# Moving the stores of one helper from SP's transfer queue to ScalarE's and GpSimd's

## The chip, the cores and the metric

The kernel runs on one core of a Trainium2 chip. A core has five engines that run their own instruction streams: TensorE (PE in the profile, with its weight loads as PEld), VectorE (DVE), ScalarE (ACT), GpSimd (POOL) and SyncE (SP). SP does no arithmetic here; it issues transfers between HBM and the on-chip buffers. ScalarE and GpSimd can issue transfers too, between their own instructions. The transfers of every issuer are carried out by the core's 16 DMA engines.

The metric is the device time of one execution in microseconds (us). Before the change three runs took 2751.06, 2753.01 and 2756.75 us; the median is 2753.01.

## The reference, cut to what matters

One layer of a hybrid encoder with 2048 tokens and a width of 1024, all in float32:

```python
xn = rms_norm(x, mix_norm_g)
proj = xn @ w_in
aq, ak, av, mq, mk, mv, mo, ipre, fpre, ga, gm = jnp.split(proj, points, axis=-1)
att = chunk_band_attention(aq, ak, av, rel_bias)          # 8 heads of 64, own chunk and 8 before it
hm = mlstm_chunkwise(silu(conv(mq)), silu(conv(mk)), mv, ipre + b_igate, fpre + b_fgate)
mlstm_out = sigmoid(mo) * rms_norm(hm, mh_norm_g)          # 4 heads of 128
y = sigmoid(ga) * (att @ w_att_proj) + sigmoid(gm) * (mlstm_out @ w_mlstm_proj)
x = x + y @ w_out
hn = rms_norm(x, ffn_norm_g)
x = x + jnp.square(jax.nn.relu(hn @ w_up)) @ w_down
return rms_norm(x, final_norm_g)
```

The large matrix products (`w_in`, `w_out`, `w_up`, `w_down`) make up most of the work.

## The kernel before

**Tiling.** The tokens stand in four blocks of 512. A tile is 128 partitions by 512 float32 values, 256 KB. For the precision of float32 every operand of a product is split into a rounded high part and a rest, and each 128 x 128 x 512 step is three matmuls (high x high, high x rest, rest x high). The large products are also built from seven smaller ones instead of eight (a Strassen-like scheme): sums and differences of operand quarters are formed, stored in HBM where they are needed again, and loaded part by part.

**What goes through HBM.** On-chip memory is small for this, so nearly every intermediate is stored and loaded again: the attention's v (`vspill`), q and k (`qfar`, `kfar`), the recurrence's inputs (`mfar`, `mvfar`), the gates (`gate`), partial sums of the input projection (`park`), the mixers' outputs (`mix`), the gated sum y (`yp`), the residual stream (`x`), the sums of operand quarters of the feed-forward's inner activations (`u`), of weights (`wsum`) and of the input (`xu`), and small rows (`mrow`, `gatepart`, `relrow`, `mid`).

**The planner.** The program is not written in the order in which it runs. Every piece of work is a Python generator that yields the engine it wants, the time it expects to take and, for transfers, a time until the data have landed: `yield "sp", 800, 2000` means 800 ns of SP's clock and landing 2000 ns later. The class `Flow` keeps a clock for each engine, picks the piece that can start earliest (then by priority), moves the engine's clock on and lets the generator write its instructions. That fixes the order in each engine's instruction stream; on the chip each stream then runs strictly in order, with semaphores for the true dependencies. So a price in a `yield` changes no instruction by itself, but it changes where that instruction and all later ones stand. `Flow.now` is a pair, the present time of the running piece and the engine on which that time came about. After a `yield "dve", ...` its second part is `"dve"`; a piece that is started by another takes over its pair; a piece that waits for an event takes the later of its own pair and the event's.

**Buffers.** The pools are small: 16 `ctx` tiles and 6 `tmp` tiles of 512 columns, 4 `wraw` tiles for raw weights, 3 `wsp` tiles for split weights, 28 `r` tiles for split operands, 8 banks of matmul results. A tile that is being stored is given back in the plan when the store has landed, and on the chip its next writer waits for that.

**The lines around the change.** `store` (L2041) is the helper for most stores. Its callers: `sum_w` (`wsum`, quarter sums of weights, after VectorE's L438), `park_u2` and `park_v` (`park`, after VectorE), `merge` (`yp`, with the queue given as `"sp!"`, which is SP at the highest priority), `evac_v` and `after_vm` (`vspill`, after VectorE's rest part; `mvfar` after an addition on VectorE), `evac_mv` (`mvfar` of blocks 0 and 1, after ScalarE), `parts` (`qfar` and `kfar`: the high part, written by ScalarE, and the rest, written by VectorE, both stored after the latter), `after_in` (`gate` and the output gate in `mfar`, after a tanh on ScalarE), `conv_far` (`mfar`, after VectorE), `take_x1` (`xu`), `after_up` through `keep` and `sums` (`u`: parts 0 and 1 are sent when ScalarE has squared them, parts 2 to 6 after VectorE's L1855 to L1864), `x2_tile` (`x`, after VectorE's L2004), `norm_mid` (`mid`), `final_keep` (`fin`), `gates_rest` (`mrow`), `gates_kept` (`gatepart`) and `table` (`relrow`).

Stores that do not use the helper: `keep` inside `quad_w` (L515, sums of weights), `keep_mix` (L1298), and the outputs (L2316 on ScalarE's queue, L2319 and L2374 on SP's).

Loads that stand in SP's queue among the stores: weights (L447, L456, L465), the parts of `u`, `xu` and `mix` (`take_u1`, L2103, split by ScalarE's L1109 and VectorE's L1114), quarters for weight sums (L433), parked sums (L769, then added by VectorE's L780), and the operands of attention and recurrence. Weights are split by ScalarE's L501 and VectorE's L503. GpSimd's own work is small: powers of small tiles (L1033, L1055, L1637, L2291, L2391), a select (L1549) and memsets (L1157, L1544).

Of the kernel before, what the change touches and what calls it, by code (L numbers as in the profile page):

```python
# [101 lines left out]
class Flow:  # L102
# [10 lines left out]
               act=dict(pe=220.0, act=130.0, dve=130.0, pool=180.0),  # L113
               dve=dict(pe=220.0, act=130.0, dve=130.0, pool=155.0), pool=dict(pe=290.0, act=130.0, dve=60.0),
               sp=dict())
# [132 lines left out]
class Layer:  # L248
# [1790 lines left out]
        fl.put(self.ctx, x)  # L2039

    def store(self, dst, src, ev, pool=None, item=None, queue="sp"):  # L2041
        yield queue, 800, 2000
        self.nc.sync.dma_start(dst, src)
        self.fl.set(ev)
        if pool is not None:
            self.fl.put(pool, item)
# [517 lines left out]
```

## Time and profile before

| | |
|---|---|
| median of three runs | 2753.01 us |
| the profiled execution | 2753.07 us |
| its span in the trace | 2751.3 us |
| HBM traffic | 458.79 MB read, 212.21 MB written |
| mean DMA rate | 245 GB/s |
| stores and loads issued on SP's queue | nearly all: 670.08 of 673.57 MB |
| ScalarE's queue | 1.06 MB |

The page gives the busy share of each engine over the whole span, and later the chain of work that ended last. Matmuls are pipelined: one 128 x 512 matmul is listed with 390 ns, but in an undisturbed stretch the next one starts about 227 ns later, so the mean time of one is not the pace. In a row of the timeline the columns are start, duration, engine, line, operation, output and inputs, and the count; "SPq" or "ACTq" is an issue of a transfer by that engine's instruction stream, which lasts until the transfer has been handed on, not until it has landed.

### The profile page before, as it was taken

What the parts mean: (1) busy time and instruction counts of PE and PEld (TensorE: products, weight loads), DVE (VectorE), ACT (ScalarE), POOL (GpSimd) and SP (SyncE); (2) the same over time, 40 slices, a digit from 0 to 9 for tenths busy, and PEclk for the clock granted to TensorE, in tenths of its full rate; (3) what the DMA queues carried; (4) which work ended last, traced back from release to release, by engine and by line L of the source; (5) the groups of instructions that cost most, each with busy time, mean ns of one, the idle gap of its engine ahead of it and who ended that gap; (6) DMA issues with size and microseconds to landing.
All of it is one profiled execution on the core that took longest, in us unless ns stands there. A gap on an engine that the chain in (4) does not pass through costs nothing.

```text
span 2751.3 us, 38074 instructions
## 1 busy us (share of the span) xinstructions
PE 2724.6 (99%) x12832; PEld 2261.5 (82%) x12832; DVE 2086.0 (76%) x3689; ACT 1526.4 (55%) x2640; POOL 44.6 (2%) x79
## 2 busy tenths in 40 slices
PE   9999999999999999999999999999999999999998
PEld 8878888788888887888888888888888888888887
DVE  7878776888775778897768889888888665667675
ACT  6545446666652434566556766657345565554443
POOL 0000000000000000000000000000000000000000
PEclk9999999999999999999999999999999999999999
DMA  8877678878877888767668778776864454588863
GB/s 295 284 254 268 234 267 281 260 235 266 255 256 254 299 305 294 244 212 260 246 237 295 254 231 223 239 257 199 294 227 171 151 205 154 180 278 281 283 230 137
DMA packets 331992, 673.57 MB, mean 245 GB/s; under 512 B 36900, under 2 KB 66468, under 8 KB 331796
## 3 DMA queue, kind: packets, MB, share of 16 engines
q1 hardware_dynamic: 331076, 670.08, 72.3%
q8 instruction: 101, 1.65, 0.2%
q10 hardware_dynamic: 720, 1.06, 0.1%
q14 instruction: 95, 0.78, 0.1%
HBM read 458.79 MB, written 212.21 MB: 244 GB/s over the span
## 4 chain that ended last, share of the span: by engine, by line
PE 83%; DVE 7%; DMA 4%; issue 3%; ACT 2%; POOL 0%; SPq 0%; POOLq 0%; DVEq 0%; ACTq 0%
PE bank L631 35%; PE bank L662 9%; PE bank L562 9%; PE bank L564 8%; PE bank L563 8%; PE bank L667 2%; PE bank L1337 2%; PE bank L1262 2%; PE bank L1369 2%; DVE wsp L503 1%; PE bank L856 1%; DVE r L1114 1%; DMA yp<-tmp 1%; DMA r<-u 1%; DVE ctx L1765 1%
## 5 line engine op out<-in xcount | busy, mean ns | idle before, releaser
L631 PE MATMUL bank<-r,wsp 128*128 128x512 f32 x4872 | 1110.9, 390 | 4.2 <-ACT r L1109 1.4
L631 PEld LDWEIGHTS bank<-r,wsp 128*128 128x128 f32 x4872 | 912.5, 188 | 198.2 <-ACT r L1109 2.1
L501 ACT CAST wsp<-wraw 128x1024 fp32r<-128x1024 f32 x439 | 461.3, 1051 | 492.1 <-PE bank L631 183.3
L503 DVE TENSOR_TENSOR wsp<-wraw,wsp 128x1024 fp32r<-128x1024 f32 x439 | 537.0, 1223 | 247.0 <-ACT wsp L501 236.7
L562 PE MATMUL bank<-r,wsp 128*128 128x512 f32 x1088 | 429.9, 396 | 0.3 <-DVE scs L1343 0.3
L564 PE MATMUL bank<-r,wsp 128*128 128x512 f32 x1088 | 425.3, 391 | 0.0
L563 PE MATMUL bank<-r,wsp 128*128 128x512 f32 x1088 | 425.2, 391 | 0.0
L662 PE MATMUL bank<-r,wsp 128*128 128x512 f32 x1512 | 370.8, 394 | 3.1 <-DVE ctx L780 2.5
L662 PEld LDWEIGHTS bank<-r,wsp 128*128 128x128 f32 x1512 | 279.4, 189 | 59.4 <-issue 2.7
L564 PEld LDWEIGHTS bank<-r,wsp 128*128 128x128 f32 x1088 | 204.3, 188 | 43.0
L562 PEld LDWEIGHTS bank<-r,wsp 128*128 128x128 f32 x1088 | 204.5, 188 | 38.4 <-DVE scs L1343 0.7
L563 PEld LDWEIGHTS bank<-r,wsp 128*128 128x128 f32 x1088 | 204.7, 188 | 38.1
L1114 DVE TENSOR_TENSOR r<-r 128x512 fp32r<-128x512 f32 x273 | 181.8, 687 | 56.8 <-ACT r L1109 55.0
L1109 ACT CAST r<-r 128x512 fp32r<-128x512 f32 x273 | 164.7, 621 | 104.4 <-DMA r<-u 77.1
L1798 DVE TENSOR_TENSOR ctx<-bank,ctx 128x512 f32<-128x512 f32 x150 | 103.0, 687 | 64.7 <-PE bank L631 63.6
L520 DVE TENSOR_TENSOR wraw<-wraw,wraw 128x1024 f32<-128x1024 f32 x112 | 136.5, 1220 | 2.2 <-DMA wsum<-wraw 1.0
L1350 ACT ACTIVATE sc<-sc,scs 128x640 f32<-128x640 f32 (+4 forms) x128 | 97.2, 760 | 54.9 <-DVE scs L1343 54.3
L1790 ACT COPY ctx<-bank 128x512 f32<-128x512 f32 x150 | 87.2, 581 | 52.0 <-PE bank L631 50.5
L2119 ACT ACTIVATE ctx<-ctx 128x512 f32<-128x512 f32 x96 | 60.5, 630 | 97.8 <-DVE ctx L1798 97.8
L1374 DVE TENSOR_TENSOR r<-bank,r 128x512 fp32r<-128x512 f32 (+1 forms) x168 | 96.4, 595 | 8.4 <-ACT r L1372 7.5
L1262 PE MATMUL bank<-r,r 128*128 128x512 f32 x336 | 95.7, 367 | 3.5 <-DVE ctx L1674 1.9
L1372 ACT CAST r<-bank 128x512 fp32r<-128x512 f32 (+1 forms) x168 | 80.7, 514 | 27.9 <-PE bank L1369 27.4
(257 smaller groups left out, 3054.1 us busy)
## 6 DMA issues: line engine op xcount, KB each, us to landing
wraw<-in_wf SPq DMA_DIRECT2D x196, 512.0 KB, 4.2
r<-u SPq DMA_DIRECT2D x224, 256.0 KB, 4.4
wraw<-wsum SPq DMA_DIRECT2D x104, 512.0 KB, 4.5
u<-ctx SPq DMA_DIRECT2D x128, 256.0 KB, 2.8
u<-tmp SPq DMA_DIRECT2D x96, 256.0 KB, 2.1
wraw<-in_w SPq DMA_DIRECT2D x47, 512.0 KB, 4.5
ctx<-in_wf SPq DMA_DIRECT2D x88, 256.0 KB, 4.2
wsum<-ctx SPq DMA_DIRECT2D x88, 256.0 KB, 3.1
```

The source lines that it names most:

```text
L501: nc.scalar.copy(w[:, 0], raw)
L503: nc.vector.tensor_sub(w[:, 1], raw, w[:, 0].bitcast(F32))
L520: V.tensor_sub(dst, x, y)
L562: mm(ps, lh, rh, start=first, stop=False)
L563: mm(ps, lh, rl, start=False, stop=False)
L564: mm(ps, ll, rh, start=False, stop=last)
L631: mm(ps, wv[:, x, k, n], a[:, y], start=new and k == 0 and x == y == 0, stop=k == 3 and x == 1, skip_group_check=True)
L662: mm(ps, wv[:, x, k, n], a[:, y], start=start and x == y == 0, stop=stop and x == 1, skip_group_check=True)
L1109: self.nc.scalar.copy(dst[:, 0], src)
L1114: self.nc.vector.tensor_sub(dst[:, 1], src, dst[:, 0].bitcast(F32))
L1262: nc.tensor.matmul(bkv[:, :, c0:c0 + w], st, sl[:, :, o:o + w], start=n == 0, stop=n == total - 1)
L1798: nc.vector.tensor_add(t[:, o:o + 512], ps, t[:, o:o + 512])
```

## The change

`store` looks at the engine on which the running piece's time came about. A store on the default queue whose piece was last on ScalarE (`"act"`) is issued on ScalarE's queue; one whose piece was last on VectorE (`"dve"`) is issued on GpSimd's; any other, and any with another queue given, stays on SP's. The planner's prices change with it: ScalarE gets an empty step with 300 ns of delay, then 60 ns and 2800 ns to landing; GpSimd gets 1000 ns and 2800 ns; SP's were 800 ns and 2000 ns.

```diff
     def store(self, dst, src, ev, pool=None, item=None, queue="sp"):
-        yield queue, 800, 2000
-        self.nc.sync.dma_start(dst, src)
+        if queue == "sp" and self.fl.now[1] == "act":
+            yield "act", 0, 300
+            yield "act", 60, 2800
+            self.nc.scalar.dma_start(dst, src)
+        elif queue == "sp" and self.fl.now[1] == "dve":
+            yield "pool", 1000, 2800
+            self.nc.gpsimd.dma_start(dst, src)
+        else:
+            yield queue, 800, 2000
+            self.nc.sync.dma_start(dst, src)
         self.fl.set(ev)
         if pool is not None:
             self.fl.put(pool, item)
```

## The prediction

> **What bounds the kernel now.** I read the page's busy shares first, then the longest pieces of the chain of waits, then windows of 100 us, and last what TensorE itself waited for.
>
> ```profile
> PE 2724.6 (99%) x12832; PEld 2261.5 (82%) x12832; DVE 2086.0 (76%) x3689; ACT 1526.4 (55%) x2640; POOL 44.6 (2%) x79
> ```
>
> The windows below end at the span, 2751.3 us, so TensorE is idle for 2751.3 - 2724.6 = 26.7 us. A busy share can hide a slow pace, so the second reading is the pace.
>
> ```profile
> 261.53 193.16 PE bank L631 x852
> ```
>
> This piece of the chain of waits is undisturbed: 193.16 / 852 = 0.227 us for a 128x512 product. The windows show whether other stretches keep that pace.
>
> ```profile
> 1000.00:1100.00 100.00, 97.68 (x431) 80.59 (x430) 74.44 (x110) 41.19 (x59) 0.00 (x0) 1.00 0.86 300
> 2300.00:2400.00 100.00, 100.00 (x443) 82.80 (x442) 62.12 (x73) 54.21 (x79) 0.00 (x0) 1.00 0.44 159
> 2700.00:2751.30 51.30, 43.93 (x210) 36.53 (x208) 25.34 (x39) 18.39 (x31) 3.19 (x5) 0.95 0.33 121
> ```
>
> The columns are stretch and length, then busy time (and count) of PE, PEld, DVE, ACT and POOL, then clock, DMA share and GB/s. 443 in 100 us is 0.226 us each; the worst stretch of long products, the first row, has 431, which is 12 x 0.227 = 2.7 us short, at a DMA share of 0.86. The granted clock is 1.00 in both. The last row holds 51.3 - 43.93 = 7.4 us of the idle time; it is the final norm, whose own DMAs do not pass through `store`. The rest is in the list of what TensorE waited for, 21 rows that add to 18.8 us (total us, times, longest):
>
> ```profile
> PE bank L662 <- DVE ctx L780: 2.5, 2, 2.3
> ...
> PE bank L631 <- ACT r L1109: 1.4, 1, 1.4
> ...
> PE bank L1337 <- DVE r L1374: 0.2, 1, 0.2
> ```
>
> So the kernel is bound by TensorE, and 18.8 us (0.7%) is about all that any better feeding could return. What can be lost has no such ceiling.
>
> **What is moved.** One line, 2043, issues every store that passes through `store`, all on SP's queue:
>
> ```profile
> L2043 SPq DMA_DIRECT2D u<-ctx x128: 319/320/792, 1197.8 to 2434.5; - x128
> L2043 SPq DMA_DIRECT2D u<-tmp x96: 319/320/1417, 1224.5 to 2434.1; - x96
> ...
> L2043 SPq DMA_DIRECT2D gate<-ctx x64: 319/320/564, 109.2 to 1098.6; - x64
> L2043 SPq DMA_DIRECT2D mfar<-ctx x48: 319/320/1237, 202.9 to 1110.7; - x48
> ...
> L2043 SPq DMA_DIRECT2D yp<-tmp x32: 319/330/650, 861.0 to 2032.1; - x32
> ...
> L2043 SPq DMA_DIRECT2D mrow<-tmp x4: 270/271/353, 171.4 to 1736.5; - x4
> ...
>   DVE ctx L438: 8.3, 6
> ...
>   DVE wsp L503: 0.2, 1
> ...
> DMA to landing us min/median/max: 2.0/3.0/7.5
> ```
>
> These are the first and the last of 19 rows, which add to 692; four `mid`, one `gatepart` and one `relrow` store make 698. The 32 `yp` stores ask for "sp!" and stay. The planner's last stamp sorts the others. To ScalarE go the gates (64), a third of `mfar` (16, the output gate), `mvfar` of blocks 0 and 1 (8), parts 0 and 1 of the seven of each `u` (2/7 of 224 = 64), `mrow` (4) and `gatepart` (1): 157. To GpSimd go 698 - 32 - 157 = 509, among them the `u` part 6 and the high halves of q and k, whose data ScalarE wrote but whose thread was last on VectorE. Nothing is removed: bytes, transfers and the waits of each store stay.
>
> **SP's queue, which gives up 666 issues.** Each is 0.32 us at the median: 213 us of issuing leave SP, and so do the waits of these stores, which hold back loads written behind them:
>
> ```profile
> SPq L456 <- DVE wsp L503: 229.5, 114, 10.0
> ...
> SPq L2043 <- ACT ctx L2123: 152.7, 80, 9.6
> ```
>
> The first row is SP waiting to load weights until VectorE has let a buffer go: the weights are ahead of their use, so an earlier turn brings nothing there. What the release can return is TensorE's waits for operands whose source is a load: L780 adds a parked tile that is loaded back, L1109 splits a tile that is loaded. They are 2.5 + 1.4 = 3.9 us. Bounds: 0, and 18.8 if all waits vanished. I take -3.9, since the other rows are waits for attention and recurrence work on VectorE and ScalarE that no load starts.
>
> **ScalarE's queue, which gets 157.** The only stores on it in this trace are four of the output:
>
> ```profile
> 2739.49 0.71 ACT L2308 ACTIVATE ctx<-ctx,r_z 128x512 f32<-128x512 f32 x1
> 2739.62 0.35 ACTq L2316 DMA_DIRECT2D out_x<-sc  x1
> 2740.11 0.58 ACT L2298 ACTIVATE tmp<-bank 128x512 f32<-128x512 f32 x1
> ```
>
> The store is issued while the next activation runs, and the one after starts 0.09 us before that ends (2739.49 + 0.71 = 2740.20): no time of ScalarE is lost. The change asks for the same shape: its empty step of 300 ns lets another activation in between. Without that cover ScalarE would wait for its own write and then issue for 0.35 us; behind it stand the casts L501 and L1109, for which L503 and L1114 on VectorE, and then TensorE, wait. Bounds: 0 to 157 x 0.35 = 55 us of an engine that is 55% busy. I take 0; the cover is there in most stages, and 55 us would raise its share only to 57%.
>
> **GpSimd's queue, which gets 509.** No DMA of GpSimd stands in the trace. The nearest row on this engine is a small tensor operation:
>
> ```profile
> L1637 POOL TENSOR_TENSOR hs<-hs,half 128x4 f32<-128x4 f32 x16 | 17.8, 1112 | 231.5 <-DVE hs L1635 194.1 <-DVE scs L1352 37.4
> ```
>
> Bounds for one issue: 0.32 us (SP's) to 1.11 us (a GpSimd instruction). As it is an instruction of that engine I take 1.11, so 0.8 us more per store before its data move; the lower bound is that a store no longer queues behind loads and lands at the 2.0 us minimum, 1.0 us earlier than the median. 509 x 1.11 = 565 us is 21% of the span: GpSimd has room. In its queue the power L1637, the select L1549 and the memsets L1157 and L1544 now stand behind stores that wait for VectorE. One store ahead of each of L1637's 16 operations costs 1.11 us of a recurrence that runs beside TensorE's other products; I count nothing for it (at most 16 x 1.11 = 18 us if no other product were ready).
>
> Which stores are late enough to be seen? The chain of waits passes through five that move, all written last by VectorE:
>
> ```profile
> 77.43 5.87 DMA vspill<-tmp
> ...
> 1006.71 5.22 DMA vspill<-tmp
> ...
> 1075.25 5.25 DMA kfar<-ctx
> ...
> 1143.79 4.60 DMA x<-ctx
> 1149.78 5.75 DMA x<-ctx
> ```
>
> Five at +0.8 us are +4.0 us (bounds -5.0 to +4.0). The chain's `yp` pieces stay on SP. Then there are the buffers: arithmetic engines waited 18 times for a store through `store` to land (the rows from L438's 8.3 us down to L503's 0.2). Each now lands 0.8 us later: 14.4 us more on VectorE and ScalarE, of which I let half, 7.2 us, reach TensorE, because three weight buffers stand between them (bounds 0 and 14.4).
>
> [...]
>
> **The sum.** -3.9 + 0 + 4.0 + 7.2 = +7.3 us. The planner gives every store other prices (60 or 1000 ns on another engine instead of 800 ns on SP), so the written order changes everywhere; that has no row. It can return at most the 18.8 us and may as well double them; I take 0 and widen the range. The profiled execution took 2753.07 us, 1.8 more than its span and equal to the median of 2753.01. Forecast: 2753 + 7 = 2760 us. About 0.2% (5.5 us) is what a measurement of this kernel can tell; the three runs spread by 5.7.
>
> **Rivals.** (1) Faster: the loads were held more than I grant. For it: SP waited 152.7 us at one kind of store alone. Against: TensorE's waits name a load's reader in 3.9 us only. If half of the 18.8 us goes, 9 us: 2744 us. (2) No change: TensorE's lead covers all, gains and delays of a few us cancel: 2753 us. For it: two of the chain's five stores lie in the window that is still 97.68% busy. Against: it is the window with the most idle time of those shown. (3) Much slower: GpSimd's queue in order. A store that waits there for VectorE holds all later ones, and the buffers they free; a store then lands not 0.8 but about 3 us later. The 18 buffer waits and five chain stores make 23 x 3 = 69 us, half of it on TensorE: 35 us, 2788 us. It decides where a wait outlasts the lead of one weight buffer, 24 products x 0.227 = 5.4 us: L438's waits are 8.3 / 6 = 1.4 us now and would be 4.4, two in a row past it. Against it: GpSimd is 2% busy, so its queue is nearly empty. (4) The sorting does not do what it says: if the stamp were "sp" for most stores, nothing would move; but each producer's last step is an arithmetic one, so I give this nothing of its own.
>
> **How the numbers follow.** Forecast 0.42, rival 1 0.22, rival 2 0.16, rival 3 0.20. The forecast's own range is 2753 to 2772 and 0.08 of its chance lies within 0.2%; of rival 1 it is 0.02. So slower is 0.34 + 0.20 = 0.54, same 0.16 + 0.08 + 0.02 = 0.26, faster 0.20. The range reaches from rival 1's centre, less 1 us, to rival 3's, plus 4 us, which leaves about half of each outside: 2743 to 2792.
>
> **What would show it.** Right: 157 issues on ScalarE's queue near 0.35 us with ScalarE's busy time unchanged; 509 on GpSimd's near 1.1 us; these landing about 0.8 us later; TensorE's busy time equal and its idle time at 26.7 + 7 = 34 us, the added waits behind `vspill`, `kfar`, `x` and reused `ctx` and `tmp`. Wrong: TensorE's idle time below 20 us (rival 1); landings 3 us later and VectorE or ScalarE waiting for stores by more than 60 us (rival 3); ScalarE's casts late behind its own stores, which would break the 0 taken there.

## The result and the profile after

| | before | after |
|---|---|---|
| median, us | 2752.66 (4 runs) | 2796.39 (4 runs) |
| lowest to highest, us | 2751.06 to 2756.75 | 2795.35 to 2804.83 |
| span of the profiled execution, us | 2751.3 | 2793.5 |

The kernel became slower by 43.7 us: the ratio is 1.0158, with a 95% interval of 1.0139 to 1.0178. The forecast was 2760 us, and the range ended at 2792.

The busy shares of the page, after:

```profile
PE 2734.8 (98%) x12832; PEld 2266.8 (81%) x12832; DVE 2079.9 (74%) x3684; ACT 1531.1 (55%) x2645; POOL 327.1 (12%) x588
```

TensorE is idle for 2793.5 - 2734.8 = 58.7 us, 32.0 more than before, and busy for 10.2 us more with the same 12832 matmuls. Together these are the 42.2 us of the span. The idle time is in the list of what TensorE waited for (us in total, times, longest), after:

```profile
PE bank L662 <- DVE ctx L780: 13.2, 4, 7.2
PE bank L631 <- DVE ctx L1798: 10.2, 5, 3.7
```

Before, the same two pairs were 2.5 and 1.1 us, so these two rows hold 19.8 of the 32.0 us. L780 and L1798 are VectorE reading results out of the matmul banks, so here TensorE waits for VectorE to empty a bank. The windows of the changed kernel (stretch and length; busy time and count of PE, PEld, DVE, ACT, POOL; clock; DMA share; GB/s) show that VectorE was not busy either:

```profile
200.00:300.00 100.00, 96.29 (x426) 79.49 (x425) 76.12 (x113) 50.06 (x79) 19.82 (x35) 0.98 0.71 247
...
1000.00:1100.00 100.00, 92.82 (x398) 76.29 (x397) 65.93 (x96) 32.90 (x48) 12.44 (x23) 0.95 0.80 277
...
2300.00:2400.00 100.00, 100.00 (x443) 82.81 (x442) 61.76 (x71) 52.75 (x76) 16.22 (x30) 1.00 0.43 153
```

Before, the first of these stretches was full:

```profile
200.00:300.00 100.00, 100.00 (x451) 83.06 (x450) 79.51 (x115) 51.74 (x82) 1.01 (x1) 1.00 0.72 263
```

In the stretch from 1000 to 1100 us 398 matmuls run where 431 ran, and VectorE and ScalarE do less too (65.93 and 32.90 us against 74.44 and 41.19): all three wait. The quiet stretch at 2300 is as before. From 1000 to 1100 us the granted clock is 0.95, against 1.00 before: 9.6 of the 10.2 us of extra busy time are lost pace at such stalls (the last section adds them up).

Who is first in that line of waits? Four views of the changed kernel around its longest stall, TensorE, VectorE, ScalarE and SP in turn (start, duration, what, and in brackets the idle time before it and what ended it):

```profile
1064.10 5.60 PE L662 MATMUL bank<-r,wsp 128*128 128x512 f32 x24
1076.88 15.44 PE L662 MATMUL bank<-r,wsp 128*128 128x512 f32 x55 [7.18 <-DVE ctx L780]
```

```profile
1072.78 0.69 DVE L1116 SCALAR_TENSOR_TENSOR r<-tmp,r 128x512 fp32r<-128x512 f32 x1 [4.52 <-ACT r L1111]
...
1076.06 0.68 DVE L780 TENSOR_TENSOR ctx<-bank,ctx 128x512 f32<-128x512 f32 x1
```

```profile
1064.09 0.63 ACT L1111 ACTIVATE r<-tmp 128x512 fp32r<-128x512 f32 x1 [4.40 <-DMA tmp<-yp]
1066.30 0.63 ACT L1111 ACTIVATE r<-tmp 128x512 fp32r<-128x512 f32 x1 [1.59 <-DMA tmp<-yp]
1072.12 0.63 ACT L1111 ACTIVATE r<-tmp 128x512 fp32r<-128x512 f32 x1 [5.18 <-DMA tmp<-yp]
```

```profile
1056.86 0.32 SPq L2051 DMA_DIRECT2D yp<-tmp  x1
1057.24 7.03 SPq L1715 DMA_DIRECT2D tmp<-yp  x3
1064.37 0.38 SPq L456 DMA_DIRECT2D wraw<-wsum  x1
```

Read from the bottom: SP stores a piece of y and, right behind it, loads y back (three loads that take it 7.03 us, of which 5.7 us are one wait for a stored piece to land); ScalarE waits for these loads, in order, 4.40 + 1.59 + 5.18 us; VectorE's L1116 waits 4.52 us for ScalarE, and the read-out L780 stands behind it; TensorE waits 7.18 us for the bank. Neither GpSimd nor ScalarE's queue is in that chain, and the `yp` stores have not moved. Why, then, did it appear?

### The profile page after: what moved, and what is told of

The parts are those of the page before. It is cut to its first block, busy times and chain, and to the rows that moved or that the text cites. A ratio compares the mean times of both kernels' runs of the same rounds, so it can differ in the third digit from the quotient of the medians.

```text
span 2793.5 us, 38435 instructions
## 1 busy us (share of the span) xinstructions
PE 2734.8 (98%) x12832; PEld 2266.8 (81%) x12832; DVE 2079.9 (74%) x3684; ACT 1531.1 (55%) x2645; POOL 327.1 (12%) x588
## 4 chain that ended last, share of the span: by engine, by line
PE 51%; issue 26%; DVE 9%; DMA 7%; POOL 5%; ACT 2%; SPq 0%; POOLq 0%; ACTq 0%; DVEq 0%
PE bank L631 17%; PE bank L562 6%; PE bank L563 6%; PE bank L564 6%; PE bank L662 5%; DVE wsp L503 2%; PE bank L1262 2%; PE bank L1369 1%; PE bank L1337 1%; DMA r<-u 1%; POOL u L2048 1%; PE bank L856 1%; DVE r L1114 1%; PE bank L667 1%; POOL wsum L2048 1%
## 5 line engine op out<-in xcount | busy, mean ns | idle before, releaser
L631 PE MATMUL bank<-r,wsp 128*128 128x512 f32 x4872 | 1117.2, 390 | 14.8 <-DVE ctx L1798 10.2
L1109 ACT CAST r<-r 128x512 fp32r<-128x512 f32 x273 | 165.3, 621 | 151.6 <-DMA r<-u 128.5
L1798 DVE TENSOR_TENSOR ctx<-bank,ctx 128x512 f32<-128x512 f32 x150 | 102.6, 686 | 61.8 <-PE bank L631 61.0
L1337 PE MATMUL bank<-r,r 128*128 128x256 f32 (+2 forms) x464 | 88.7, 311 | 1.9 <-DMA r<-qfar 1.9
```

What stands on the lines that cost most here:

```text
L631: mm(ps, wv[:, x, k, n], a[:, y], start=new and k == 0 and x == y == 0, stop=k == 3 and x == 1, skip_group_check=True)
L1109: self.nc.scalar.copy(dst[:, 0], src)
L1337: nc.tensor.matmul(bk[:, :c1 - c0], q[:, y, i * P:(i + 1) * P], kf[:, f * P + c0:f * P + c1], start=y == 0, stop=y == 1)
```

## The experiments

Ten kernels were run; each ratio is to the kernel before on the same chip, with a 95% interval.

| run | what leaves SP | order of the instructions | median, us (runs) | ratio |
|---|---|---|---|---|
| e1_act_only | 157 to ScalarE | the build's, new prices | 2765.44 (6) | 1.0034 [1.0022, 1.0047] |
| e2_pool_only | 509 to GpSimd | the build's, new prices | 2795.06 (4) | 1.0136 [1.0115, 1.0156] |
| e3_plan_only | nothing | the build's, new prices | 2778.28 (4) | 1.0078 [1.0061, 1.0094] |
| e4_queues_only | 157 and 509 | the build's, old prices | 2798.71 (4) | 1.0159 [1.0144, 1.0174] |
| e5_pinned_queues | 157 and 509 | held as before, all engines | 2760.76 (10) | 1.0025 [1.0014, 1.0037] |
| e6_pinned_act | all 666 to ScalarE | held as before, all engines | 2775.03 (4) | 1.0072 [1.0051, 1.0093] |
| e7_pinned_pool | 509 to GpSimd | held as before, all engines | 2758.33 (10) | 1.0018 [1.0006, 1.0030] |
| e8_pinned_157 | 157 to ScalarE | held as before, all engines | 2756.95 (11) | 1.0010 [0.9999, 1.0022] |
| e9_pinned_sp | 157 and 509 | held on SP only | 2774.63 (6) | 1.0080 [1.0064, 1.0097] |
| e11_free_sp | 157 and 509 | held on all but SP | 2778.64 (4) | 1.0088 [1.0072, 1.0105] |

The first four tested two theories. P: the planner's new prices (60 or 1000 ns instead of 800 on SP) put the whole program in a worse order. Q: the transfers themselves, issued elsewhere, land later or hold other work.

**e1_act_only: ScalarE's branch alone.** The branch for GpSimd falls to the old one:

```diff
-        elif queue == "sp" and self.fl.now[1] == "dve":
-            yield "pool", 1000, 2800
-            self.nc.gpsimd.dma_start(dst, src)
```

> Only the 157 stores whose piece was last on ScalarE move, with the changed kernel's prices; the 509 others stay on SP. Theory P (the plan: SP's clock no longer carries the stores, so loads and what reads them are written too early): 157 of 666 prices leave SP, so about a quarter of the loss, 2753 + 10 = 2763 us, more where SP was full. Theory Q (the queues: stores land later from GpSimd and share the DMA engines out of turn): GpSimd has nothing, so 2753 us within 5.

Measured: 1.0034, some 9 us.

**e2_pool_only: GpSimd's branch alone.** The same with the other branch left out:

```diff
-        if queue == "sp" and self.fl.now[1] == "act":
-            yield "act", 0, 300
-            yield "act", 60, 2800
-            self.nc.scalar.dma_start(dst, src)
-        elif queue == "sp" and self.fl.now[1] == "dve":
+        if queue == "sp" and self.fl.now[1] == "dve":
```

> Only the 509 stores whose piece was last on VectorE move to GpSimd, with the changed kernel's prices. Theory P: three quarters of the prices leave SP, about 2753 + 33 = 2786 us. Theory Q: GpSimd's stores are the cause, all of it, about 2796 us.

Measured: 1.0136, some 37 us. The 509 stores on GpSimd bring most of the loss; by themselves these two runs do not say how.

**e3_plan_only: the new prices, but SP issues everything.**

```diff
-            self.nc.scalar.dma_start(dst, src)
+            self.nc.sync.dma_start(dst, src)
...
-            self.nc.gpsimd.dma_start(dst, src)
+            self.nc.sync.dma_start(dst, src)
```

> The changed kernel's prices, so the written order of every engine as in the changed kernel, but all stores are issued by SP. Theory P: the order makes the loss: 2790 to 2805 us, and more if SP's real queue is now behind its planned clock. Theory Q: without the other queues the time is as before, 2750 to 2760 us.

Measured: 1.0078, some 21 us, with no transfer moved: another order alone can cost half of the loss. (It is not quite the order of the changed kernel, for a reason that e4 brings out.)

**e4_queues_only: the new queues, but the old prices.**

```diff
+        by = {"act": self.nc.scalar, "dve": self.nc.gpsimd}.get(self.fl.now[1], self.nc.sync)
+        if queue != "sp":
+            by = self.nc.sync
         yield queue, 800, 2000
-        self.nc.sync.dma_start(dst, src)
+        by.dma_start(dst, src)
```

> The prices and so the order of the kernel before (SP's clock, 800 and 2000 ns), but the stores are issued by ScalarE (157) and GpSimd (509). Theory P: 2748 to 2758 us, as before or a little faster because loads no longer stand behind stores. Theory Q: the queues make the loss: 2785 to 2800 us.

Measured: 1.0159, the whole loss without any new price. So P is not needed for a loss of this size, though e3 shows that the new prices by themselves can cost 21 us. Q seemed to stand, until the instruction streams of e4 were laid beside those of before. Although the planner did the same, the streams differ. In the programs that the two kernels build, without the moved stores and the semaphore instructions, 210 of TensorE's 12515 instructions stand in another order, 251 of VectorE's 3694, 161 of ScalarE's 2434 and 239 of the 1598 that SP keeps. The planner does not have the last word, as the description of the kernel before had it: the build places every engine's instructions once more, by its own model of when they are ready, and in the kernel before SP's instructions already stand up to 183 places from where the planner put them. A store that leaves SP changes that model's picture, and with it the order of loads and arithmetic that nobody edited. So two new theories. O: the re-written order costs the time. H: the hardware does (landing times, shared DMA engines, GpSimd's queue in order).

**e5_pinned_queues: the new queues in the old order.** The prices are the old ones; every instruction other than the moved stores is chained to the one that stood ahead of it on its engine before. A list of shifts from the planner's order carries that order:

```diff
+        by = self.fl.now[1] if queue == "sp" else "sp"
         yield queue, 800, 2000
-        self.nc.sync.dma_start(dst, src)
+        self.moving = by in ("act", "dve")
+        {"act": self.nc.scalar, "dve": self.nc.gpsimd}.get(by, self.nc.sync).dma_start(dst, src)
+        self.moving = False
...
+            for e, count in COUNTS.items():
+                got = pinned[e]
+                row = [got[k + shift[at + k]] for k in range(count)]
+                at += count
+                for a, b in zip(row, row[1:]):
+                    tc.add_manual_dep(b, a.name, mybir.DependencyInfo(
+                        mybir.DependencyClass.NoSync, mybir.DependencyReason.DATA), reason="order")
```

> The order of the kernel before is pinned on every engine: all matmuls, all work of VectorE, ScalarE and GpSimd and all loads of SP stand exactly as before; only the 666 stores are issued by ScalarE (157) and GpSimd (509). Theory O (when the stores leave SP, the build writes the loads and their readers in another order, and that order loses): 2748 to 2762 us. Theory H (the transfers themselves: stores of GpSimd land later, and three queues share the DMA engines): 2785 to 2800 us, as the unpinned run with the same prices (2798.7).

Measured: 1.0025, 7 us (4 to 10 by the interval). The same 666 stores from the same two queues, and 37 us of the 44 are gone. The stretches that stalled, in the windows of e5:

```profile
200.00:300.00 100.00, 100.00 (x450) 83.07 (x449) 79.74 (x116) 51.05 (x81) 20.07 (x36) 1.00 0.72 261
...
1000.00:1100.00 100.00, 99.61 (x440) 82.18 (x439) 74.62 (x111) 40.39 (x58) 12.60 (x24) 1.00 0.86 302
```

They are full, with GpSimd issuing as much as in the changed kernel. In the program that e5 builds, every instruction other than the moved stores stands where it stood before. O holds, and H keeps 7 us. Strictly this takes e4 apart, which has the old prices. The changed kernel has the new prices as well; how its own 44 us divide between the order of the prices, the order of the build and the queues was not measured.

**e6_pinned_act and e7_pinned_pool: one queue each, in the old order.** Against e5 only the choice of the queue differs:

```diff
-        {"act": self.nc.scalar, "dve": self.nc.gpsimd}.get(by, self.nc.sync).dma_start(dst, src)
+        (self.nc.scalar if by in ("act", "dve") else self.nc.sync).dma_start(dst, src)
```

```diff
-        {"act": self.nc.scalar, "dve": self.nc.gpsimd}.get(by, self.nc.sync).dma_start(dst, src)
+        (self.nc.gpsimd if by == "dve" else self.nc.sync).dma_start(dst, src)
```

> The same pinned order, but all 666 stores go from ScalarE's queue and none from GpSimd. Theory O: 2748 to 2762 us if ScalarE can carry 666 issues; ScalarE waits for VectorE's results in its own order, so up to 20 us more. Theory H with GpSimd's way of issuing as the cause: near 2753 to 2770 us. Theory H with the second queue as such as the cause: 2785 us or more.

> The same pinned order; the 509 stores go from GpSimd, the 157 of ScalarE stay on SP in their old places. Theory O: 2748 to 2762 us. Theory H: GpSimd's part of the loss, 2780 to 2795 us.

Measured: 1.0072 with all 666 on ScalarE, 1.0018 with 509 on GpSimd. So GpSimd's queue is the cheaper one for these 509 (the other 157 alone cost 0.10% on ScalarE's, in e8). A likely reason, argued and not tested by itself: on ScalarE the casts for the next products stand behind a store that waits for VectorE, on GpSimd little does (in e6 the arithmetic of the two is 1525.0 and 45.6 us).

**e8_pinned_157: only ScalarE's share, in the old order.** The stores that stay on SP are not chained in e7 and e8; 13 of SP's instructions in e7 and 30 in e8 stand elsewhere than before.

```diff
-        {"act": self.nc.scalar, "dve": self.nc.gpsimd}.get(by, self.nc.sync).dma_start(dst, src)
+        (self.nc.scalar if by == "act" else self.nc.sync).dma_start(dst, src)
```

> All five engines keep the order of before; only the 157 stores that ScalarE wrote last leave from ScalarE's queue, the other 509 stay on SP's. Theory O (the re-written order costs about 36 us of the 44, the queues themselves about 7): of the 7 us the 509 on GpSimd alone cost 2758.3 - 2752.6 = 5.8, so these 157 cost 1 to 3 us or nothing: 2752 to 2757 us, no difference that can be told. Rival H (a store issued by ScalarE holds its casts): 157 x 0.33 us is 51 us of ScalarE, half of it seen: 2770 us or more, as the 2775 of all 666 on ScalarE would suggest. A gain of 3 us or more (2750 or less) would say that SP's queue was in the way and the order had hidden it.

Measured: 1.0010 with an interval that takes in 1, against 1.0034 for the same 157 stores in e1, where the order was free and the prices new. No gain came to light: no version here beats the kernel before.

**e9_pinned_sp and e11_free_sp: whose order is it?** In both, the loop of e5 over the engines leaves some out:

```diff
 # e9_pinned_sp
+                if e != "SP":
+                    continue
 # e11_free_sp
+                if e == "SP":
+                    continue
```

> Planner's prices of before, 157 stores on ScalarE's queue and 509 on GpSimd's; SP's remaining transfers are held to the order they had before, the other engines are written as the build likes. Theory O-SP (what costs is that SP's loads stand in another order, weights ahead of activations): nearly all of the order's 36 us comes back: 2760 to 2770 us. Rival O-compute (what costs is the new order on TensorE, VectorE and ScalarE): 2785 to 2800 us. In between says that both orders have to fit each other.

> The counterpart: planner's prices of before, 157 stores on ScalarE's queue and 509 on GpSimd's; TensorE, VectorE, ScalarE and GpSimd are held to the order of before, and SP's loads are written as the build likes. Theory O-SP: the loads stand in the new order, so most of the loss stays: 2780 to 2800 us. Rival O-compute: 2758 to 2768 us, as with all five orders held (2760.8).

Measured: 1.0080 and 1.0088, between the two theories' numbers for e9 and just under O-SP's for e11: neither has it alone. The four kernels with both new queues and old prices make a square:

| | other engines' order of before | other engines' order by the build |
|---|---|---|
| SP's order of before | 1.0025 (e5) | 1.0080 (e9) |
| SP's order by the build | 1.0088 (e11) | 1.0159 (e4) |

SP's loads in the new order cost 0.63% (17 us) and the arithmetic engines in theirs 0.55% (15 us), each uncertain by some 0.2%. With the 7 us of e5 that makes 39 of e4's 44 us; the rest is within the uncertainty. The division is a rough one, since the build places what is left free anew in each kernel: 65 of SP's 1598 instructions stand elsewhere in e11 than in e4, and 19 of TensorE's 12515 in e9. The losses also have their places. The windows of e11, then those of e9:

```profile
200.00:300.00 100.00, 96.31 (x421) 79.38 (x419) 76.12 (x109) 50.95 (x82) 18.54 (x33) 0.97 0.70 249
...
1000.00:1100.00 100.00, 92.10 (x400) 75.81 (x400) 66.10 (x97) 34.06 (x49) 12.50 (x23) 0.97 0.82 278
```

```profile
200.00:300.00 100.00, 100.00 (x451) 83.06 (x450) 79.53 (x115) 52.32 (x83) 18.92 (x35) 1.00 0.74 261
...
1000.00:1100.00 100.00, 99.28 (x438) 81.92 (x437) 74.46 (x111) 38.47 (x54) 13.29 (x25) 1.00 0.87 306
```

The stalls of the changed kernel at 200 to 300 and 1000 to 1100 us come with SP's new order alone (e11) and are absent where SP keeps its old one (e9). The loss of e9 lies elsewhere, in many small waits; its largest ones:

```profile
PE bank L1371 <- ACT sc L1359: 5.3, 7, 1.7
PE bank L633 <- DVE ctx L1800: 4.7, 2, 2.8
PE bank L1618 <- DVE cst L1622: 3.2, 1, 3.2
```

(Line numbers of the held kernels are two higher than those of before, so these are L1357, L1798 and L1620.)

### Where SP's new order loses

One place, seen in SP's timeline around 207 us, first before and then e4:

```profile
206.20 0.33 SPq L447 DMA_DIRECT2D wraw<-in_wf  x1
...
207.21 0.38 SPq L1046 DMA_DIRECT2D tmp<-in_x  x1
...
210.18 0.33 SPq L447 DMA_DIRECT2D wraw<-in_wf  x1
212.26 5.46 SPq L1046 DMA_DIRECT2D tmp<-in_x  x2
```

```profile
206.47 5.70 SPq L447 DMA_DIRECT2D wraw<-in_wf  x2
212.22 6.10 SPq L1046 DMA_DIRECT2D tmp<-in_x  x2
```

In e4 two weight loads stand together, the second waits 5.0 us for a free weight buffer, and the activation load that before was issued between them, at 207.21, goes out after 212.22. ScalarE's L1048 behind it waits longer, 3.99 us against 2.14, and L1958 stands behind that L1048 (in e4 at 217.87 us, before at 212.14). On VectorE L1965 waits for L1958 (at this place 1.09 us before and 1.74 in the changed kernel), and the read-out L1798 stands behind L1965. TensorE, which before runs 77 matmuls there without a gap, stops 2.99 us for L1798. Before, then e4 (ScalarE, then TensorE, in each):

```profile
211.51 0.63 ACT L1048 ACTIVATE tmp<-tmp 128x512 f32<-128x512 f32 x1 [2.14 <-DMA tmp<-in_x]
...
214.69 17.62 PE L631 MATMUL bank<-r,wsp 128*128 128x512 f32 x77
```

```profile
217.24 0.63 ACT L1048 ACTIVATE tmp<-tmp 128x512 f32<-128x512 f32 x1 [3.99 <-DMA tmp<-in_x]
...
225.22 10.95 PE L631 MATMUL bank<-r,wsp 128*128 128x512 f32 x47 [2.99 <-DVE ctx L1798]
```

The second kind of loss: a load that reads back a store, or overwrites a tile that is being stored, now comes up before that store has landed. What SP waited for, in the changed kernel (two lines of loads; us, times, longest):

```profile
SPq L433 <- DMA wsum<-ctx: 56.4, 17, 9.1
...
SPq L433 <- DMA u<-ctx: 41.0, 6, 11.0
...
SPq L769 <- DMA mfar<-ctx: 26.4, 9, 5.2
...
SPq L769 <- DMA park<-ctx: 22.4, 10, 5.0
...
SPq L769 <- DMA gate<-ctx: 18.0, 10, 3.5
```

Before, the same waits:

```profile
SPq L769 <- DMA park<-ctx: 7.4, 7, 2.1
...
SPq L769 <- DMA mfar<-ctx: 6.7, 3, 3.6
...
SPq L769 <- DMA gate<-ctx: 3.7, 3, 2.2
...
SPq L433 <- DMA u<-ctx: 3.3, 3, 1.3
...
SPq L433 <- DMA wsum<-ctx: 2.8, 3, 1.7
```

The rows of SP's waits that name a transfer, added up, give 179 us (137 times) before, 518 (220) after, 575 (238) in e11, 397 (182) in e5 and 392 (181) in e9. SP's queue, relieved of 666 issues, ran ahead of the stores that left it, and then stood still for their landings, with everything behind it. Such waits by themselves cost little here (e5 has 397 us of them and loses 7 us); that it costs where the build has put an urgent load behind it is a reading of single places, not a measurement. Nor is it needed for a loss: e3, where no store left SP, has 181 us of such waits (129 times), as before, and loses 21 us. The load of the parts of `u`, for which ScalarE's L1109 waits, shows that, before and after:

```profile
ACT r L1109 <- DMA r<-u: 77.1, 64, 3.9
```

```profile
ACT r L1109 <- DMA r<-u: 128.5, 81, 6.1
```

In e5 it is 93.3 us, in e11 131.6, in e9 103.4: it goes with SP's order. What stays open is why the build's model prefers this order once the stores have left; no kernel here changes the model. That the order alone, in the old queues, loses the same was not tried, save with the order that the new prices give (e3).

## Why the prediction was wrong, step by step

- **The sorting** came out as counted: 157 issues from ScalarE's queue (L2045) and 509 from GpSimd's (L2048). Rival 4 falls.
- **ScalarE's queue, taken at 0, held.** An issue lasts 0.326 us; e8 cannot be told from before. The cover is not without limit: with all 666 there (e6) the loss is 0.72%, 20 us.

```profile
L2045 ACTq DMA_DIRECT2D gate<-ctx x64: 325/326/389, 111.4 to 1123.0; - x64
```

- **GpSimd's queue.** One issue takes 0.54 us, inside the bounds of 0.32 and 1.11 but half of the value taken; GpSimd is busy for 327.1 us, not 44.6 + 565. The stores do land later, at a median of 4.0 us against 3.0 (of all 698 before), which is +1.0 where +0.8 was taken. From issue to landing the `u<-tmp` stores alone went from 2.1 to 3.5 us. The two terms made of it, +4.0 and +7.2, came out at 5 us together in e7 (2 to 8 by its interval).

```profile
L2048 POOL DMA_DIRECT2D u<-tmp x96: 539/539/551, 1251.1 to 2474.6; - x96
...
DMA to landing us min/median/max: 2.1/4.0/10.0
```

- **SP's release, taken at -3.9, was not seen.** No kernel in the old order gained: e7 and e8 are 5 and 3 us slower by their medians' ratios, not faster. The waits behind loads grew, as the row of L1109 shows.
- **The sum of these steps**, +7.3 us, is what e5 measures for the same edit with the order held (+7). That the total fits is in part luck: a gain of 3.9 us that did not come and the 3 us by median of ScalarE's share (e8, not told from 0) make up for the 6 us too much that were counted for GpSimd.
- **The step that failed** is the last one: "the written order changes everywhere; that has no row. It can return at most the 18.8 us and may as well double them; I take 0". A new order costs some 37 us (e4 against e5, on the same queues), twice the upper bound given for it. Its cause was seen only in part: the prediction put the new order down to the planner's prices. These do cost 21 us when SP issues everything (e3), but e4 has a new order, and the whole loss, without a new price, because the build places the instructions again. How much of the changed kernel's own loss each of the two makes stays open. And an order was counted as if good and bad luck were even. The order of before left TensorE idle for 26.7 us of 2751.3, so there was little to win and much to lose; each of the five new orders tried here (e1 to e4 and the change itself) loses.
- **"TensorE's busy time equal"** failed: +10.2 us, 9.6 of them from the clock after stalls.
- **Rival 3** (2788 us) was nearest in time, and one of its marks was met: VectorE and ScalarE waited 74.5 us for moved stores (24.4 before), as a total above the 60 named, though the rise is 50. But its mechanism is not the cause: the landings are 1 us later, not 3, and GpSimd's queue in the old order costs 5 us (e7), not 35. Rivals 1 and 2 fall with the time.

## What to carry to other kernels

Where a build places the instructions by a model of its own, moving a transfer to another queue can change the order on every engine: lay the new streams beside the old ones before reasoning about queues, and hold the order fixed to measure the queue by itself. In a kernel whose bounding engine is 99% busy, a new order is no even bet, and "no row for it" should be priced by how much there is to lose. Here SP's queue, freed of 666 stores, did not become free (518 us of waits for transfers, 179 before): look at which stores the remaining loads will now catch up with.

## What the runs showed of the hardware that was not expected

**A stall cost more than its length here.** In the rows of the longest stall above, of 7.18 us, the 24 matmuls ahead of it take 5.60 us and the 55 behind it 15.44; less the 0.39 us of the last one that is 0.227 us each and then 0.279. Shorter stalls did it as well. Windows of 10 us of the changed kernel (same columns as above), and TensorE's row for the second:

```profile
220.00:230.00 10.00, 6.29 (x21) 4.72 (x20) 7.77 (x14) 5.48 (x8) 0.54 (x1) 0.83 0.41 156
560.00:570.00 10.00, 8.14 (x36) 6.36 (x35) 7.71 (x25) 5.21 (x14) 1.65 (x2) 0.86 0.67 199
...
1510.00:1520.00 10.00, 9.30 (x47) 7.86 (x48) 8.48 (x28) 5.91 (x11) 0.20 (x1) 1.00 1.04 357
```

```profile
566.89 2.68 PE L662 MATMUL bank<-r,wsp 128*128 128x512 f32 x6 [1.86 <-DVE tmp L1275]
```

A clock of 0.83 over 10 us is 1.7 us of lost pace. The second place has 0.86 in its window and 0.97 in the next, which is 1.7 us again; the six matmuls of its row, less the 0.39 us of the last one, are 0.458 us apart, twice the 0.227. There are six such places up to 1330 us (at 220, 560, 950, 1070, 1120 and 1320 us) where before has one in the same part of the span (0.83 at 740 us, after a wait of 1.89 us); five at 1.7 us and the 2.8 us that the 55 matmuls lost, less one, make 9.6 of the 10.2 us by which TensorE's busy time grew. The stalls of these five lasted 1.86 to 3.88 us. The stall of 1.91 us at 1510 (L1337, waiting for `qfar`) left the clock at 1.00, so what decides between two stalls of equal length is not shown.

**What the issuing engine changes.** A store took GpSimd 0.54 us to issue, ScalarE 0.326 and SP 0.32, and with the same order of instructions the `u<-tmp` stores landed at a median of 3.5 us from GpSimd (e5), 2.5 from ScalarE (e6) and 2.4 from SP (e8). The `wsum<-ctx` stores show half of that gap: 3.7, 3.3 and 3.2 us. So these two kinds of stores landed 1.1 and 0.5 us later from GpSimd than from SP.
